# Experts' gates added up by scatters into a zeroed DRAM matrix and multiplied in at the second products, in place of one-hot tables and gate products

## The chip, the cores and the metric

The kernel runs on one core of a Trainium2 chip. The metric is the time of one execution on the device in microseconds (us), the median of several runs. TensorE does the matrix products, VectorE and ACT (ScalarE) the elementwise work, POOL (GpSimd) is almost idle and issues some of the transfers, and SP issues the loads of the weights.

## The reference, cut to what matters

The reference is one transformer block on 256 tokens of width 2048: a gated delta net and a sparse attention side by side, a mixing of the two, and then a layer of 16384 experts (PEER), of which each token uses 16 for each of 8 heads. Only the last part matters here:

```python
qh = (xb @ wq).reshape(TB, PEER_HEADS, PEER_QDIM)
s1 = einsum('thd,hkd->thk', qh[..., :half], keys1)     # 128 scores
s2 = einsum('thd,hkd->thk', qh[..., half:], keys2)     # 128 scores
v1, i1 = top_k(s1, 16); v2, i2 = top_k(s2, 16)
cand = v1[..., :, None] + v2[..., None, :]             # 16 x 16
sc, pos = top_k(cand, 16)
eidx = i1 * 128 + i2, taken at pos                     # which of 16384 experts
gw = softmax(sc)                                       # the gates
act = gelu(einsum('td,thkd->thk', xb, u[eidx]))
out = einsum('thk,thkd->td', gw * act, v[eidx])
```

The kernel gathers no experts. It computes the first product of every token with all 16384 experts, the gelu of each, multiplies by a matrix of gates G (zero for an expert that a token doesn't use, the sum of the gates where two heads choose the same one), and multiplies the result with all of `v`.

## The kernel before

An expert has the number 128 i + j. The first products run in 128 groups j: a group is the 128 experts i on the partitions and 256 tokens in the columns, and its sum over 2048 is 48 matmuls (`stat256`; each weight is split into a high and a low part in a format of TensorE, three products for each of 16 slices). The gelu of group j goes to `at_j(j)`, a piece of 128 x 256 of the big tile `A` (two tiles, groups 0 to 79 and 80 to 127). The second products read `A` as weights (`w_split` cuts each group into `wh` and `wl`) and stream `v`, in two halves of 1024 output columns, 128 groups j in each half, 12 matmuls of 512 columns in a group.

All weights come as 512 KB loads on SP's queue. Each load is cut into two pieces; ACT casts the high part of a piece (`whi`) and VectorE subtracts (`wlo`), up to three pieces ahead of TensorE (class `Stream`). Each engine runs its instructions in the order in which the program writes them. The order around the main loop is made while the program is written out: a class `Background` holds generators (tasks), and `bg.step()`, called after each group of matmuls, lets each task whose time has come write out its next few instructions. The times belong to a simple clock of planned costs (`Times`); a task yields the time at which it wants to go on, a negative value meaning just that time and not at least half a microsecond after its last instruction. At most 8 tasks are active.

Routing is such a task (`route_task`, line 1762): for each head the scores, `top16` on 128 and on 256 values, and after the last head one pass that turns the positions into the numbers i and j of the experts and the scores into gates. Then i, j and gates are transposed (tokens in the columns) with `PE.transpose`, and the gates are split into three bf16 parts.

`gate_task` (line 1854) makes the matrix of gates on TensorE, four tokens at a time. VectorE builds for each token two tables of 128 x 128 bf16: `oi`, which has a one where the choice (on the partitions) has the number i, and `ow`, the same for j, times the three parts of the gate. Three matmuls for each token sum `oi` against `ow` into 128 x 128 gates in PSUM. `put` multiplies them into the groups of `A` that are there already, or stores them in `A` where the group isn't there yet; in that case the gelu goes to a tile `aj`, and VectorE multiplies it in. This runs beside the first products, from the end of routing (about 1340 us) to the end of that stage; `need("gates")` stands behind the loop.

During the second products `g2_task` computes a row of the modulation on VectorE (64 steps of one load and one `SCALAR_TENSOR_TENSOR` of 512 columns), and then loads it, `x1` and the last norm's weights on POOL's queue.

All instructions that go through the timing wrapper carry its line, 289, in the profile; they are told apart by the names of their tiles.

Of the kernel before, what the change touches and what calls it, by code (L numbers as in the profile page):

```python
# [18 lines left out]
T = 256  # L19
# [48 lines left out]
def _const_array():  # L68
    t = np.arange(128)
    ch = t // 64  # L70
    same = ch[:, None] == ch[None, :]
    parts = []

    def add(name, a):
        a = np.asarray(a, np.float32).reshape(128, -1)
        _CONSTS[name] = (sum(p.shape[1] for p in parts), a.shape[1])
        parts.append(a)

    add("ident", np.eye(128))
    add("iota", np.repeat(t[None, :], 128, 0))  # L80
    add("sel", t % 32 == 0)
    add("one", np.ones(128))
    add("ones", np.ones((128, 128)))
    add("tri", same & (t[:, None] <= t[None, :]))
    add("same", same)
    add("ind0", np.repeat((t < 64)[:, None], 128, 1))
    add("ind1", np.repeat((t >= 64)[:, None], 128, 1))

    i, j = t[:, None] % 64, np.arange(64)[None, :]
    add("identc", i == j)  # L90

    add("inclTd", (ch[:, None, None] == np.arange(2)[None, :, None]) & (i[:, :, None] <= j[:, None, :]))
    for l in range(6):
        b = 1 << l
        add(f"lev{l}", (i // (2 * b) == j // (2 * b)) & (i // b % 2 == 1) & (j // b % 2 == 0))
    add("causal", np.where(t[None, :] <= t[:, None], 0.0, NEG))
    n = np.arange(16)
    for tb in range(2):
        add(f"cmpm{tb}", np.where(16 * n[None, :] + 31 <= (t + 128 * tb)[:, None], 0.0, NEG))
    add("cmpv", np.stack([t >= 31, t + 128 >= 31], 1))  # L100
    add("selc", t[:, None] % 32 == np.arange(32)[None, :])
    half = 16
    inv = (np.float32(500000.0) ** (-np.arange(half, dtype=np.float32) / np.float32(half))).astype(np.float32)
    add("inv", np.repeat(inv[None, :], 128, 0))
    return np.concatenate(parts, 1)
# [74 lines left out]
NPAIR = 3  # L180
WO = [(512 * j, 512) for j in range(4)]
# [224 lines left out]
def _build(nc, tc, A, out, stacks, dump, at, stop_at):  # L406
# [33 lines left out]
    bg = Background(times, 8, lambda: "first" in done and next(ada_gen, None), lambda: PACE2 if "o7" in done else PACE)  # L440
# [108 lines left out]
    crowd = dram.tile([1, D], F32, name="crowd")  # L549

# [701 lines left out]
    bg.add(pre_task())  # L1252
    def kc_task():
        yield from kv_rot(c0, 64, kcT[:, 0], 1)
        done.add("kc")
# [455 lines left out]
    sp = pool(st_A, "sp", side=RIGHT)  # L1711
    st_e = stack()
# [23 lines left out]
    eqs = [qs_[:, 1024 * i:1024 * i + 1024] for i in range(2)]  # L1736
# [9 lines left out]
    gate = tmp(256)  # L1746
    eidx = tmp(512).rearrange("p (w b n) -> p w b n", w=2, b=2)

    ij = [ep.tile([128, T], BF, name=f"ij{n}") for n in range(2)]
    gs = [ep.tile([128, T], BF, name=f"gs{n}") for n in range(3)]  # L1750
    iota4 = ep.tile([128, 128, 4], BF, name="iota4")
    V.tensor_copy(iota4, C("iota")[:, :, None].to_broadcast([128, 128, 4]))
# [9 lines left out]
    def route_task():  # L1762
# [24 lines left out]
        V.tensor_copy(iif, ii)  # L1787
        V.tensor_scalar(au, posu, 4, None, op0=OP.logical_shift_right)
        V.tensor_copy(af[:, 0], au)
        V.tensor_scalar(au, posu, 15, None, op0=OP.bitwise_and)  # L1790
        V.tensor_copy(af[:, 1], au)
        yield bg.now() + RPACE
        for tb in range(2):
            for w in range(2):
                for h0 in (0, 4):
                    hs_ = slice(h0, h0 + 4)
                    eq = eqs[w].rearrange("p (h s k) -> p h s k", h=4, s=16)
                    V.tensor_tensor(eq, af[:, w, tb, hs_, :, None].to_broadcast([128, 4, 16, 16]),
                                    C("iota")[:, None, None, 0:16].to_broadcast([128, 4, 16, 16]), OP.is_equal)
                    yield bg.now() + RPACE  # L1800
                    V.tensor_tensor(eq, eq, iif[:, tb, w, hs_, None, :].to_broadcast([128, 4, 16, 16]), OP.mult)
                    yield bg.now() + RPACE
                    V.tensor_reduce(eidx[:, w, tb, :].rearrange("p (h s) -> p h s", h=8)[:, hs_], eq, axis=AX.X,
                                    op=OP.add)
                    yield bg.now() + RPACE
        for tb in range(2):
            V.tensor_tensor(gw[:, tb], scv[:, tb], scv[:, tb, :, 0:1].to_broadcast([128, 8, 16]), OP.subtract)
        yield bg.now() + RPACE
        act(gw, gw, AF.Exp)
        yield bg.now() + RPACE  # L1810
        sm = vv[:, 0, 0, :, 0:2].rearrange("p h b -> p b h")
        V.tensor_reduce(sm, gw, axis=AX.X, op=OP.add)
        V.reciprocal(sm, sm)
        V.tensor_tensor(gw, gw, sm[:, :, :, None].to_broadcast([128, 2, 8, 16]), OP.mult)
        yield bg.now() + RPACE
        for dst, src in zip((*ij, gate), (eidx[:, 0], eidx[:, 1], gw.rearrange("p b h s -> p b (h s)"))):
            S.copy(dst, transpose_to(ps(), src, 2).rearrange("p b t -> p (b t)"))
            yield bg.now() + RPACE
        for n in range(3):
            V.tensor_copy(gs[n], gate)  # L1820
            if n < 2:
                V.tensor_tensor(gate, gate, gs[n], OP.subtract)
        done.add("gate")
# [26 lines left out]


    j_there, t_there = 0, 0

    def gate_task():
        nonlocal t_there
        nt = 4
        yield from wait_for("gate")
        ones, sums = {}, {}
        start, steps = bg.now(), 0
        pace = ((128 - j_there) * 5.15 - GEND) / (4 * T / nt)  # L1860

        def pause():
            nonlocal steps
            steps += 1
            return start + steps * pace

        def make(t0):
            oi = ep.tile([128, 128, nt], BF, name="oi", bufs=2)
            ow = ep.tile([128, 3, 128, nt], BF, name="ow", bufs=2)
            over = lambda a: a[:, None, t0:t0 + nt].to_broadcast([128, 128, nt])  # L1870
            V.tensor_tensor(ow[:, 2], iota4, over(ij[1]), OP.is_equal)
            V.tensor_tensor(oi, iota4, over(ij[0]), OP.is_equal)
            yield -pause()
            for n in range(3):
                V.tensor_tensor(ow[:, n], ow[:, 2], over(gs[n]), OP.mult)
            ones[t0] = oi, ow

        def products(t0):
            oi, ow = ones.pop(t0)
            p = ps()  # L1880
            for t in range(nt):
                for n in range(3):
                    PE.matmul(p[:, 128 * t:128 * t + 128], oi[:, :, t], ow[:, n, :, t], start=n == 0, stop=n == 2)
            sums[t0] = p

        def put(t0):
            nonlocal t_there
            pv = sums.pop(t0).rearrange("p (t j) -> p j t", t=nt)
            for q, (a, b) in enumerate(((0, JA), (JA, 128))):
                m = min(max(j_there, a), b)  # L1890
                x = act_by[q][:, :, t0:t0 + nt]
                if m > a:
                    V.tensor_tensor(x[:, :m - a], x[:, :m - a], pv[:, a:m], OP.mult)
                if m < b:
                    S.copy(x[:, m - a:], pv[:, m:b])
            t_there = t0 + nt

        yield from make(0)
        yield pause()
        for t0 in range(0, T, nt):  # L1900
            if t0 + nt < T:
                yield from make(t0 + nt)
                yield -pause()
            if t0:
                put(t0 - nt)
            yield pause()
            products(t0)
            yield pause()
        put(T - nt)
        done.add("gates")  # L1910

    bg.add(gate_task())
    for j in range(128):
        if j == JA:
            need("gate")
        p = ps()
        for i in range(4):
            h, l = stream.get()
            stat256(p[:, :T], h, l, 4 * i, 4)
        a = at_j(j)  # L1920
        n = t_there
        if n:
            t = ep.tile([128, T], F32, name="aj", bufs=2)
            act(t[:, :n], p[:, :n], AF.Gelu_apprx_tanh)
            V.tensor_tensor(a[:, :n], a[:, :n], t[:, :n], OP.mult)
        if n < T:
            act(a[:, n:], p[:, n:T], AF.Gelu_apprx_tanh)
        j_there = j + 1
    need("gates")
# [5 lines left out]
    vp_ = lambda: hp.tile([128, 1024], F32, name="ht")  # L1935
    ssf = sp.tile([128, 2, 4], F32, name="ssf")
# [10 lines left out]
    def g2_task():  # L1947
# [5 lines left out]
        for m, v in enumerate(ada_late((G2,), lambda q: crow[q // 2][:, q % 2 * 512:q % 2 * 512 + 512],  # L1953
                                       small[:, 0:64].rearrange("p (n q) -> p n q", q=4), small[0:16, 128:256],
                                       lambda m: room[:, m % 2 * 512:m % 2 * 512 + 512])):
            yield max(start + G2PACE * m, v or 0.0)
# [7 lines left out]
    bg.add(g2_task())  # L1964

# [59 lines left out]
    V.memset(ssf, 0.0)  # L2025
    ws = [w_split(j) for j in range(AHEAD)]
    for half in range(2):
        accs = [[ps() for c in range(2)] for tb in range(2)]
        for j in range(126 if half else 128):
            w = ws.pop(0)  # L2030
            if j + AHEAD < 128 or half == 0:
                ws.append(w_split((j + AHEAD) % 128))
            for n in range(2):
# [42 lines left out]
```

## Time and profile before

| | |
|---|---|
| median of 3 runs | 2703.28 us (2698.82 to 2706.44) |
| profiled execution | 2697.54 us, its span 2695.8 us |
| busy, share of the span | TensorE 98%, VectorE 73%, ACT 52%, POOL 1% |
| granted clock of TensorE | 0.995 of full speed |
| moved by DMA | 571.15 MB, 212 GB/s over the span |

The profile is that of one execution. A busy TensorE is counted from a matmul's start to its modelled end, so overlapping matmuls count once. "Idle before" is the time that an engine stood still ahead of an instruction, with what ended it. The time of a transfer is that from its issue to its landing.

### The profile page before, as it was taken

What the parts mean: (1) busy time and instruction counts of PE and PEld (TensorE: products, weight loads), DVE (VectorE), ACT (ScalarE), POOL (GpSimd) and SP (SyncE); (2) the same over time, 40 slices, a digit from 0 to 9 for tenths busy, and PEclk for the clock granted to TensorE, in tenths of its full rate; (3) what the DMA queues carried; (4) which work ended last, traced back from release to release, by engine and by line L of the source; (5) the groups of instructions that cost most, each with busy time, mean ns of one, the idle gap of its engine ahead of it and who ended that gap; (6) DMA issues with size and microseconds to landing.
All of it is one profiled execution on the core that took longest, in us unless ns stands there. A gap on an engine that the chain in (4) does not pass through costs nothing.

```text
span 2695.8 us, 46915 instructions
## 1 busy us (share of the span) xinstructions
PE 2648.1 (98%) x17004; PEld 2278.1 (85%) x17004; DVE 1958.4 (73%) x4378; ACT 1393.3 (52%) x2983; POOL 36.6 (1%) x83
## 2 busy tenths in 40 slices
PE   8999999999999999999999999999999999999998
PEld 5777777777877778999999999999988888788886
DVE  6667877767777777999866666677577777766666
ACT  4446756565555445454544444444455555555555
POOL 0001000000000000000000000000000000000000
PEclk9999999999999999999999999999999999999999
DMA  9886756666676885555544444444577777765554
GB/s 348 310 313 229 243 174 199 197 225 229 226 241 234 291 311 200 177 173 187 185 160 152 155 157 157 153 157 155 179 256 235 235 234 235 251 193 189 188 188 157
DMA packets 176921, 571.15 MB, mean 212 GB/s; under 512 B 20048, under 2 KB 20384, under 8 KB 176176
## 3 DMA queue, kind: packets, MB, share of 16 engines
q1 hardware_dynamic: 168336, 538.21, 60.5%
q0 software_dynamic: 6624, 23.65, 2.5%
q10 hardware_dynamic: 1728, 6.29, 0.6%
q8 instruction: 133, 2.18, 0.3%
q14 instruction: 100, 0.82, 0.1%
HBM read 554.94 MB, written 13.13 MB: 211 GB/s over the span
## 4 chain that ended last, share of the span: by engine, by line
PE 91%; DVE 4%; ACT 2%; DMA 2%; issue 1%; ACTq 0%; DVEq 0%; POOLq 0%
PE ps L289 91%; DVE wlo L289 1%; DMA adas<-ada_t 1%; ACT whi L289 1%; DVE adas L289 0%; DMA raw<-w_in 0%; DVE cv L289 0%; ACT L289 0%; DVE ht L289 0%; DMA ccom<-consts 0%; DVE x L289 0%; ACT gsq L289 0%; DVE big L289 0%; ACT mix L289 0%; ACT o L289 0%
## 5 line engine op out<-in xcount | busy, mean ns | idle before, releaser
L289 DVE TENSOR_TENSOR wlo<-raw,whi 128x512 fp32r<-128x512 f32 (+2 forms) x1632 | 1098.2, 685 | 509.6 <-ACT whi L289 476.9
L289 ACT CAST whi<-raw 128x512 fp32r<-128x512 f32 (+2 forms) x1632 | 994.4, 618 | 772.7 <-PE ps L289 600.6
L289 PE MATMUL ps<-ht,whi 128*128 128x256 f32 x4608 | 828.8, 282 | 0.8 <-DVE ht L289 0.8
L289 PEld LDWEIGHTS ps<-ht,whi 128*128 128x128 f32 x4608 | 708.1, 189 | 1.2 <-DVE ht L289 1.0
L289 PE MATMUL ps<-ht,wlo 128*128 128x256 f32 x2304 | 647.2, 281 | 0.0
L289 PE MATMUL ps<-whi,ht 128*128 128x512 f32 (+2 forms) x1536 | 523.0, 403 | 5.0 <-ACT whi L289 3.8
L289 PEld LDWEIGHTS ps<-ht,wlo 128*128 128x128 f32 x2304 | 434.1, 188 | 0.0
L289 PE MATMUL ps<-wlo,wh 128*128 128x512 f32 x1024 | 408.6, 399 | 0.0
L289 PE MATMUL ps<-whi,wh 128*128 128x512 f32 x1024 | 403.7, 394 | 0.8 <-ACT wh L289 0.8
L289 PE MATMUL ps<-whi,wl 128*128 128x512 f32 x1024 | 401.5, 392 | 0.0
L289 PEld LDWEIGHTS ps<-whi,ht 128*128 128x128 f32 x1536 | 289.6, 190 | 87.3 <-issue 10.8
L289 PE MATMUL ps<-wlo,ht 128*128 128x512 f32 (+2 forms) x768 | 300.8, 392 | 3.4 <-DVE wlo L289 3.0
L289 PEld LDWEIGHTS ps<-whi,wh 128*128 128x128 f32 x1024 | 192.2, 188 | 50.8 <-ACT wh L289 1.0
L289 PEld LDWEIGHTS ps<-whi,wl 128*128 128x128 f32 x1024 | 192.2, 188 | 46.3 <-DVE wl L289 0.2
L289 PEld LDWEIGHTS ps<-wlo,wh 128*128 128x128 f32 x1024 | 192.2, 188 | 44.0
L289 PEld LDWEIGHTS ps<-wlo,ht 128*128 128x128 f32 x768 | 146.5, 191 | 32.3 <-DVE wlo L289 8.2
L289 ACT CAST wh<-A 128x256 fp32r<-128x256 f32 x256 | 103.7, 406 | 134.4 <-PE ps L289 134.4
L289 DVE SCALAR_TENSOR_TENSOR adas<-adas,crow 128x512 f32<-128x512 f32 x192 | 131.6, 686 | 43.1 <-DMA adas<-ada_t 42.8
L289 DVE TENSOR_TENSOR wl<-A,wh 128x256 fp32r<-128x256 f32 x256 | 109.0, 427 | 65.7 <-ACT wh L289 65.4
L289 PE MATMUL ps<-ow,oi 128*128 128x128 bf16 x768 | 101.3, 296 | 0.0
L289 ACT COPY A<-ps 128x192 f32<-128x192 f32 (+16 forms) x124 | 34.4, 307 | 114.1 <-DVE A L289 93.3
L289 PEld LDWEIGHTS <-oi 128*128 128x128 bf16 x768 | 81.7, 118 | 3.8
(323 smaller groups left out, 2298.6 us busy)
## 6 DMA issues: line engine op xcount, KB each, us to landing
raw<-u SPq DMA_DIRECT2D x256, 512.0 KB, 3.5
raw<-v SPq DMA_DIRECT2D x256, 512.0 KB, 3.6
raw<-w_in SPq DMA_DIRECT2D x170, 512.0 KB, 4.4
adas<-ada_t SPq DMA_DIRECT2D x192, 256.0 KB, 3.6
raw<-ada_w SPq DMA_DIRECT2D x64, 512.0 KB, 6.5
raw<-wn SPq DMA_DIRECT2D x32, 512.0 KB, 4.9
raw<-wo SPq DMA_DIRECT2D x32, 512.0 KB, 4.9
raw<-wq SPq DMA_DIRECT2D x32, 512.0 KB, 3.5
```

The source lines that it names most:

```text
L289: r = f(*args, **kw)
```

## The change

A DRAM matrix `gated[tb]` of 128 i x 128 j x 128 tokens takes the place of the tables, one for each block of 128 tokens. A new background task, `zero_task`, fills both with zeros from a zeroed tile, in 64 writes of 256 KB on ACT's queue, 5 us of the planner's clock apart. Nine tasks may be active.

Routing now finishes two heads at a time (`settle`, `NSET = 2`): numbers, gates, and for each choice its place (i x 128 + j) x 128 + token. Then `indirect_dma_start` on POOL's queue adds one gate for each of the 128 tokens of a block to its place, 32 choices x 2 blocks after each two heads, 256 in all. The transposes, the three bf16 parts, `gate_task` and its tables are gone, and each gelu goes straight to `A`.

Ahead of the second products `gates_load` starts to load the gates of two groups j at a time on POOL's queue (two loads of 128 KB, three tiles in turn). In their first half `gate_mult` multiplies them into two groups of `A` on VectorE, one to two groups ahead of `w_split`, and issues the load for six groups on. `g2_task` yields a fixed next time, at least 2 us later, instead of one behind its last instruction.

```diff
+ZPACE = 5.0
+NGT = 3
+NSET = 2
-    bg = Background(times, 8, lambda: "first" in done and next(ada_gen, None), lambda: PACE2 if "o7" in done else PACE)
+    bg = Background(times, 9, lambda: "first" in done and next(ada_gen, None), lambda: PACE2 if "o7" in done else PACE)
+    gated = [dram.tile([128, 128, 128], F32, name=f"gated{tb}") for tb in range(2)]
+    def zero_task():
+        zero = per.tile([128, 512], F32, name="zero")
+        V.memset(zero, 0.0)
+        for js in range(0, 128, 4):
+            for g in gated:
+                S.dma_start(g[:, js:js + 4].rearrange("i j t -> i (j t)"), zero)
+                yield bg.now() + ZPACE
     bg.add(pre_task())
+    bg.add(zero_task())
...
+    def gates_load(j):
+        g = sp.tile([128, 2, 2, 128], F32, name="gates2", bufs=NGT)
+        for tb in range(2):
+            G.dma_start(g[:, tb], gated[tb][:, j:j + 2])
+        gates_of.append(g)
...
+            if h % NSET == NSET - 1:
+                yield from settle(slice(h - NSET + 1, h + 1))
+                done.add(f"settled{h}")
+        done.add("gate")
+    def settle(hs_):
...
+        for tb in range(2):
+            for w in range(2):
+                eq = eqs[w].rearrange("p (h s k) -> p h s k", h=NSET, s=16)
+                V.tensor_tensor(eq, af[:, w, tb, hs_, :, None].to_broadcast([128, NSET, 16, 16]),
+                                C("iota")[:, None, None, 0:16].to_broadcast([128, NSET, 16, 16]), OP.is_equal)
+                V.tensor_tensor(eq, eq, iif[:, tb, w, hs_, None, :].to_broadcast([128, NSET, 16, 16]), OP.mult)
+                V.tensor_reduce(eidx[:, w, tb, :].rearrange("p (h s) -> p h s", h=8)[:, hs_], eq, axis=AX.X,
+                                op=OP.add)
+                yield bg.now() + RPACE
...
+        i, j = eidx[:, 0, :, ns], eidx[:, 1, :, ns]
+        V.scalar_tensor_tensor(i, i, 128.0, j, op0=OP.mult, op1=OP.add)
+        V.tensor_scalar(i, i, 128.0, C("tcol"), op0=OP.mult, op1=OP.add)
+        V.tensor_copy(place[:, :, ns], i)
         yield bg.now() + RPACE
-        for dst, src in zip((*ij, gate), (eidx[:, 0], eidx[:, 1], gw.rearrange("p b h s -> p b (h s)"))):
-            S.copy(dst, transpose_to(ps(), src, 2).rearrange("p b t -> p (b t)"))
-            yield bg.now() + RPACE
...
+        for n in range(ns.start, ns.stop):
+            for tb in range(2):
+                nc.gpsimd.indirect_dma_start(
+                    gated[tb].rearrange("i j (t o) -> (i j t) o", o=1),
+                    bass.IndirectOffsetOnAxis(ap=place[:, tb, n:n + 1], axis=0),
+                    gate[:, tb, n:n + 1], None, compute_op=OP.add)
...
-    def gate_task():
...
-    bg.add(gate_task())
     for j in range(128):
...
-        a = at_j(j)
-        n = t_there
-        if n:
-            t = ep.tile([128, T], F32, name="aj", bufs=2)
-            act(t[:, :n], p[:, :n], AF.Gelu_apprx_tanh)
-            V.tensor_tensor(a[:, :n], a[:, :n], t[:, :n], OP.mult)
-        if n < T:
-            act(a[:, n:], p[:, n:T], AF.Gelu_apprx_tanh)
-        j_there = j + 1
-    need("gates")
+        act(at_j(j), p[:, :T], AF.Gelu_apprx_tanh)
     st_e.close()
...
+    for j in range(0, 2 * NGT, 2):
+        gates_load(j)
...
-            yield max(start + G2PACE * m, v or 0.0)
+            yield -max(start + G2PACE * m, bg.now() + 2.0, v or 0.0)
...
+    def gate_mult(j):
+        a = act_by[j >= JA][:, j - JA * (j >= JA):j - JA * (j >= JA) + 2, :].rearrange("p j (b t) -> p b j t", b=2)
+        V.tensor_tensor(a, a, gates_of[j // 2], OP.mult)
+        if j + 2 * NGT < 128:
+            gates_load(j + 2 * NGT)
...
+    gate_mult(0)
+    gate_mult(2)
     ws = [w_split(j) for j in range(AHEAD)]
     for half in range(2):
...
             if j + AHEAD < 128 or half == 0:
                 ws.append(w_split((j + AHEAD) % 128))
+            if half == 0 and j % 2 and j + 3 < 128:
+                gate_mult(j + 3)
```

## Rows read from the trace of the kernel before

**Rows 1.** The page: busy times by engine, and the chain of waits.

```profile
PE 2648.1 (98%) x17004; PEld 2278.1 (85%) x17004; DVE 1958.4 (73%) x4378; ACT 1393.3 (52%) x2983; POOL 36.6 (1%) x83
...
PE 91%; DVE 4%; ACT 2%; DMA 2%; issue 1%; ACTq 0%; DVEq 0%; POOLq 0%
```

**Rows 2.** Stretches: length, busy us and starts by engine, clock, DMA share, GB/s.

```profile
50.00:100.00 50.00, 49.84 (x325) 35.55 (x325) 33.53 (x64) 19.42 (x36) 0.00 (x0) 1.00 0.93 357
205.00:570.00 365.00, 352.17 (x2661) 275.23 (x2661) 279.09 (x791) 228.32 (x548) 10.03 (x30) 0.98 0.64 208
1150.00:1250.00 100.00, 100.00 (x849) 100.00 (x849) 92.65 (x302) 49.94 (x92) 0.00 (x0) 1.00 0.56 177
1250.00:1340.00 90.00, 90.00 (x763) 90.00 (x763) 74.09 (x109) 47.31 (x86) 0.00 (x0) 1.00 0.59 188
1340.00:1440.00 100.00, 100.00 (x847) 99.33 (x847) 65.72 (x146) 45.00 (x107) 0.00 (x0) 1.00 0.49 158
1967.00:2324.00 357.00, 356.94 (x1530) 287.04 (x1531) 269.25 (x511) 198.34 (x385) 0.00 (x0) 1.00 0.73 240
```

**Rows 3.** Groups by form: count, busy us, mean ns, idle time before.

```profile
L289 DVE TENSOR_TENSOR wlo<-raw,whi 128x512 fp32r<-128x512 f32 x1600 | 1083.9, 689 | 502.4 <-ACT whi L289 470.0 <-PE ps L289 0.3
...
L289 PE MATMUL ps<-ow,oi 128*128 128x128 bf16 x768 | 101.3, 296 | 0.0
...
L289 DVE TENSOR_TENSOR ow<-ow,gs 128x512 bf16<-128x512 bf16 x192 | 75.4, 421 | 2.2
...
L289 DVE TENSOR_TENSOR oi<-iota,ij 128x512 bf16<-128x512 bf16 x64 | 26.8, 419 | 0.0
```

**Rows 4.** Timeline of TensorE: start, duration in us, instruction.

```profile
1894.79 1.58 PE L289 MATMUL ps<-ow,oi 128*128 128x128 bf16 x12
1896.12 0.48 PE L289 MATMUL ps<-ht,whi 128*128 128x256 f32 x2
```

**Rows 5.** Tile A: ns min/median/max, first and last start in us.

```profile
L289 ACT CAST wh<-A x256: 388/406/407, 1966.6 to 2677.0; 128x256 fp32r<-128x256 f32 x128
...
L289 DVE MAX8 A<-A x96: 284/295/429, 1082.7 to 1252.2; 128x8 f32<-128x128 f32 x64, 128x8 f32<-128x256 f32 x32
...
L289 DVE TENSOR_TENSOR A<-A,ccom x8: 1217/1219/1223, 1257.6 to 1316.1; 128x1024 f32<-128x1024 f32 x8
...
L289 PE MATMUL ps<-ccom,A x6: 270/272/273, 1331.5 to 1337.0; 128*128 128x128 f32 x6
```

**Rows 6.** Timeline of POOL, as rows 4, with the idle time before.

```profile
205.71 0.50 POOL L289 DMA_DIRECT2D crowd<-crow  x1
...
1962.22 1.06 POOL L289 DMA_DIRECT2D ht<-crowd  x2 [890.47 <-PE ps L289]
```

**Rows 7.** Tile mixd, as rows 5: writes on ACT's queue.

```profile
L289 ACTq DMA_DIRECT2D mixd<-mix x12: 326/326/347, 476.9 to 846.0; - x12
```

**Rows 8.** DMA issues: count, KB each, median us from issue to landing.

```profile
x1d<-x POOLq DMA_DIRECT2D x8, 256.0 KB, 3.7
ht<-x1d POOLq DMA_DIRECT2D x4, 512.0 KB, 10.3
...
cw<-cw POOLq DMA_DIRECT2D x1, 256.0 KB, 5.8
...
modr<-adarow POOLq DMA_DIRECT2D x1, 8.0 KB, 3.8
modr<-ht POOLq DMA_DIRECT2D x1, 8.0 KB, 1.6
```

**Rows 9.** Tile ht in the second products, as rows 5.

```profile
L289 DVE SCALAR_TENSOR_TENSOR ht<-ht x64: 684/684/686, 1977.2 to 2325.7; 128x512 f32<-128x512 f32 x64
```

**Rows 10.** What TensorE waited for: us in total, times, longest.

```profile
PE ps L289 <- ACT wh L289: 0.8, 1, 0.8
```

**Rows 11.** Timeline of VectorE beside POOL's issues, as rows 4.

```profile
1961.58 0.69 DVE L289 TENSOR_TENSOR wlo<-raw,whi 128x512 fp32r<-128x512 f32 x1
1962.61 0.69 DVE L289 TENSOR_TENSOR wlo<-raw,whi 128x512 fp32r<-128x512 f32 x1 [0.34 <-ACT whi L289]
```

More of the change, by code (lines that the diff above doesn't have):

```diff
@@ L82, in _const_array @@
     add("one", np.ones(128))
+    add("tcol", t)
     add("ones", np.ones((128, 128)))
@@ L1711, in _build @@
     sp = pool(st_A, "sp", side=RIGHT)
+    gates_of = []
+    def gates_load(j):
[3 more added lines that the diff above has]
+        gates_of.append(g)
     st_e = stack()
@@ L1735, in _build @@
     qhs = [qs_[:, 256 * i:256 * i + 256] for i in range(16)]
-    eqs = [qs_[:, 1024 * i:1024 * i + 1024] for i in range(2)]
+    eqs = [qs_[:, NSET * 256 * i:NSET * 256 * (i + 1)] for i in range(2)]
     work = [[tmp(512) for _ in range(4)]]
@@ L1745, in _build @@
     gw = tmp(256).rearrange("p (b h s) -> p b h s", b=2, h=8)
-    gate = tmp(256)
     eidx = tmp(512).rearrange("p (w b n) -> p w b n", w=2, b=2)
[L1749 to L1752, printed above, removed]
+    place = ep.tile([128, 2, 128], U32, name="place")
+    gate = ep.tile([128, 2, 128], F32, name="gate")
     MIN = -3.0e38
@@ L1786, in route_task @@
                 yield bg.now() + RPACE
[L1787 to L1791, printed above, removed]
+            if h % NSET == NSET - 1:
[3 more added lines that the diff above has]
+    def settle(hs_):
+        V.tensor_copy(iif[:, :, :, hs_], ii[:, :, :, hs_])
+        V.tensor_scalar(au[:, :, hs_], posu[:, :, hs_], 4, None, op0=OP.logical_shift_right)
+        V.tensor_copy(af[:, 0, :, hs_], au[:, :, hs_])
+        V.tensor_scalar(au[:, :, hs_], posu[:, :, hs_], 15, None, op0=OP.bitwise_and)
+        V.tensor_copy(af[:, 1, :, hs_], au[:, :, hs_])
         yield bg.now() + RPACE
@@ L1794, in route_task @@
             for w in range(2):
[L1795 to L1799, printed above, removed]
-                    yield bg.now() + RPACE
[L1801 to L1805, printed above, removed]
+                eq = eqs[w].rearrange("p (h s k) -> p h s k", h=NSET, s=16)
@@ L1806, in route_task @@
         for tb in range(2):
-            V.tensor_tensor(gw[:, tb], scv[:, tb], scv[:, tb, :, 0:1].to_broadcast([128, 8, 16]), OP.subtract)
+            V.tensor_tensor(gw[:, tb, hs_], scv[:, tb, hs_], scv[:, tb, hs_, 0:1].to_broadcast([128, NSET, 16]),
+                            OP.subtract)
         yield bg.now() + RPACE
-        act(gw, gw, AF.Exp)
+        act(gw[:, :, hs_], gw[:, :, hs_], AF.Exp)
         yield bg.now() + RPACE
-        sm = vv[:, 0, 0, :, 0:2].rearrange("p h b -> p b h")
@@ L1812, in route_task @@
-        V.tensor_reduce(sm, gw, axis=AX.X, op=OP.add)
+        ns = slice(16 * hs_.start, 16 * hs_.stop)
+        sm = vv[:, 0, 0, hs_, 0:2].rearrange("p h b -> p b h")
+        V.tensor_reduce(sm, gw[:, :, hs_], axis=AX.X, op=OP.add)
         V.reciprocal(sm, sm)
-        V.tensor_tensor(gw, gw, sm[:, :, :, None].to_broadcast([128, 2, 8, 16]), OP.mult)
-        yield bg.now() + RPACE
-        for dst, src in zip((*ij, gate), (eidx[:, 0], eidx[:, 1], gw.rearrange("p b h s -> p b (h s)"))):
-            S.copy(dst, transpose_to(ps(), src, 2).rearrange("p b t -> p (b t)"))
-            yield bg.now() + RPACE
@@ L1819, in route_task @@
[L1819 to L1823, printed above, removed]
+        V.tensor_tensor(gate[:, :, ns].rearrange("p b (h s) -> p b h s", s=16), gw[:, :, hs_],
+                        sm[:, :, :, None].to_broadcast([128, 2, NSET, 16]), OP.mult)
+        i, j = eidx[:, 0, :, ns], eidx[:, 1, :, ns]
+        V.scalar_tensor_tensor(i, i, 128.0, j, op0=OP.mult, op1=OP.add)
+        V.tensor_scalar(i, i, 128.0, C("tcol"), op0=OP.mult, op1=OP.add)
@@ L1847, in _build @@
             done.add(f"qh{ct // 2}")
-    j_there, t_there = 0, 0
-    def gate_task():
[L1855 to L1910, printed above, removed]
-    bg.add(gate_task())
     for j in range(128):
```

## The prediction

> **What bounds the kernel now.** First the page's busy times and its chain of waits: TensorE is busy 2648.1 of 2695.8 us, and the chain of work that ended last lies on it for 91% [rows 1]. Then the table of stretches, for the two stages that the change touches. While the first products run (the 128 groups j of `stat256`, about 1145 to 1966 us), TensorE has no idle time and starts 849 matmuls per 100 us before the gates' products begin, 847 once they are mixed in; VectorE is busy 92.7% in one of these stretches and TensorE loses nothing by it. In the second products, the half that will carry the new multiplications (1967 to 2324 us) has TensorE busy 356.9 of 357 us, VectorE 269.3, ACT 198.3, DMA 0.73 [rows 2]. So a matmul taken out of the first stage is worth its slot, and work taken off VectorE or ACT there is worth nothing; work added to VectorE in the second stage costs nothing as long as the cover holds.
>
> **What goes.** The gates' products are 768 matmuls of 128x128 bf16 [rows 3]. Their slot is read from the stretches: 847 starts in 100 us without idle time give 0.118 us for each matmul, of either kind [rows 2], so 768 x 0.118 = 90.7 us. One group of 12 began at 1894.79 us and the matmul behind it at 1896.12, 0.111 us each [rows 4], which would give 85; the group's busy column says 101.3 [rows 3], but there modelled ends lie over the next matmul. I take 90.7, with 85 and 101 as ends. The six transposes of gates and indices [rows 5] go too, 6 x 0.118 = 0.7 us. On VectorE the tables and gate products (x192, x64 for `oi` and as many for `ow`, at 0.42 us: 134 us) [rows 3] and the multiplications from PSUM go; by the above that is worth 0.
>
> **What is added, in the order in which it runs.**
>
> Zeroing: 64 writes of 256 KB, issued on ACT's queue, one per 5 us of the planner's clock, from where the setup loads on POOL's queue stand now (205.7 us) [rows 6]. A write issued there takes ACT 0.326 us [rows 7], so 64 x 0.326 = 20.9 us of ACT, in a stretch (205 to 570 us) where ACT is busy 228 and TensorE 352 of 365 us, DMA 0.64 [rows 2]. Ends: 0, if ACT's free 137 us take them, and 21, if each one delays TensorE's chain. ACT is mostly free, so nearer to 0: I take +3. The ninth place among the background tasks shifts the order of work in this stage, to either side; I allow 5 us for it.
>
> Routing: `settle` runs four times instead of once. It is the same comparison, product and sum over 16 candidates, 48 operations of 512 elements instead of 24 of 1024 (1.22 us each) [rows 5]. The nearest row for the half width is 0.689 us [rows 3], so 33 us instead of 29, and there are some 40 small ones, taken at no more than the 0.28 us of the shortest MAX8 [rows 5]: about +10 us of VectorE over 250. Three of 512 elements are now issued back to back (2.1 us); a `top16` already is five operations of up to 0.43 us [rows 5]. Cost on TensorE between 0 and 8 us; +1.
>
> Scatters: 256 on POOL's queue, 128 elements of 4 bytes each. POOL had been idle for 890 us at 1962.22 [rows 6], so nothing is queued behind them but the gates' loads. A scatter that adds into a matrix must find the sums of the one before, so I expect each to wait until the last one on its own matrix has landed; two matrices alternate, which makes 128 steps of one landing time each. Nothing in this trace is a scatter. Nearest rows: POOL's two small writes to DRAM land after 1.6 and 3.8 us, its 256 KB writes after 3.7; the far end is 10.3 us for 512 KB reads [rows 8]. I take 3.7, as two of the three rows of writes have about that. Start: first and last MAX8 are at 1082.7 and 1252.2 us [rows 5], so a head takes 21.3 us, the second head ends at 1125 and its settle some 20 us later: 1145. Then 1145 + 128 x 3.7 = 1619 us. The second products begin at 1966.6 now (first cast to `wh`) [rows 5], then at 1966.6 - 91.4 = 1875; less 5.8 us for a load of gates (256 KB on POOL's queue) [rows 8] the sums are due at 1869. Cover: 250 us. It is gone at (1869 - 1145) / 128 = 5.7 us per step.
>
> The Trainium skill, DMA: Bandwidth & Descriptors, section "Anatomy of one DMA — SWDGE (gpsimd) path", puts the fixed part of such a DMA at about 2.0 us; by that (an estimate) the chain takes 256 us, and the sum stays as it is. Rows 8 are mostly higher, and I go by them.
>
> Gates' loads: 128 of 128 KB on POOL's queue, 0.53 us of POOL each (1.06 for two) [rows 6], two for every 5.6 us of the first half. Three buffers give some 16 us of lead against 5.8 to 10.3 us to land [rows 8]. DMA goes from 0.73 by 16.8 MB in 357 us (47 on 240 GB/s) to about 0.87, where 0.93 with 357 GB/s left TensorE at 49.84 of 50 us [rows 2]. Taken as 0.
>
> Multiplications: 64 on VectorE, 128x512 f32, 0.689 us each as the split has it [rows 3]: 44 us, so 269 + 44 = 313 of 357, 88%. The G2 task may now run faster than its 5.5 us per step (64 steps from 1977.2 to 2325.7) [rows 9]; at 4.75 us VectorE stands at about 90% for 305 us. The cover is the stretch with 92.7% and a full TensorE [rows 2]. Ends: 0 and 44; I take +1. At the stage's start the first multiplications can run before the last gelu ends, so the 0.8 us that TensorE waits there for `wh` [rows 10] stays.
>
> **Sum.** -90.7 - 0.7 + 3 + 1 + 1 = -86.4 us. The profiled execution took 2697.5 us (span 2695.8), so 2611. The median of the three runs is 2703.3, 5.7 us above it, and I carry that over: 2617 us. What a measurement of this kernel can tell from no change is about 0.3%, 8 us. With the ends of the slot (85 to 101), of the zeroing (0 to 21) and the planner's 5 us, the forecast's own range is 2602 to 2635.
>
> **Rivals.**
>
> (a) The chain of scatters sets the start of the second products. One mechanism, on POOL's queue: while sums are missing the loads of gates wait, VectorE waits for the first load, and TensorE for VectorE. It decides from 5.7 us per step; with a step of P the whole takes 2617 + 128 (P - 5.7). At 6.4 us the gain is gone. At 7 us: 2783; if both matrices make one chain of 256 at 3.7 us (7.4 per step): 2835. For it: no scatter is in this trace, 10.3 us exists as a landing time [rows 8], and 128 separate elements may land later than one block. Against: all the rows of writes are under 4 us. Chance 0.12 that no gain is left (0.10 beyond 0.3%), 0.04 for a delay that leaves some.
>
> (b) VectorE's cover breaks where it is thinnest, in the routing. From 1145 to 1340 us some 53 steps, 106 scatters, run beside a VectorE with about 23 us free (7.4 per 100 us, later 15.9 of 90) [rows 2]. If each scatter kept VectorE out for as long as POOL takes for a plain issue (0.53 us), that is 56 us, and with the 10 us of settle 43 more than there is: 2660 us. A sign against: at 1962.22 POOL issued two loads in 1.06 us, and the split that VectorE began at 1962.61 took 0.69 us, as the one before it did [rows 6, 11]. But these loads read no indices. Chance 0.11.
>
> The Trainium skill, SBUF — State Buffer, section "Who interferes with whom", has this as a rule: a VectorE instruction with two SBUF inputs and a GpSimd instruction that reads SBUF shut each other out for the whole instruction. The split has two such inputs. Rows 11 agree only in so far as a plain issue doesn't shut it out; no run here shows an issue that reads indices.
>
> (c) The zeroing lies on the path whole: 18 us over the forecast, 2635. For it: TensorE already has 13 us idle in 205 to 570 us, so chains over other engines do reach it there [rows 2]. Against: ACT is 63% busy there. Chance 0.06.
>
> (d) The multiplications in the second products lie on the path whole, by late loads or a full VectorE: 43 over the forecast, 2660. Against: the cover worked out above. Chance 0.05.
>
> That leaves 0.62 for the forecast. Faster by over 0.3% are the forecast, (b), (c), (d) and the part of (a) that leaves a gain: 0.88. The rest of (a) gives 0.10 for slower and 0.02 between. The range for 8 in 10, 2600 to 2662, takes in (b) to (d) and leaves most of (a) out.
>
> **What would show it.** The first products end near 1875 us with the same 849 matmuls per 100 us, and no matmul of `oi` and `ow` is left. POOL shows 256 scatters, the last one well before that end (near 1619 us by my step); if they lie further apart than 5.7 us per pair, and the first multiplication waits for a load, (a) is right. Splits longer than 0.69 us beside scatters, and TensorE under 849 per 100 us up to 1340 us, would be (b); the stage before 570 us longer by more than 5 us, (c); TensorE idle in the first half of the second products, (d). I am wrong above all if a scatter's landing time is far from that of a plain write.

## The result, and the profile after

The changed kernel takes 2619.03 us (median of 4 runs, 2615.24 to 2621.55) against 2702.89 us for the kernel before in the same rounds (2698.82 to 2706.44): a ratio of 0.9689, 95% interval 0.9670 to 0.9708. Forecast were 2617 us and a range of 2600 to 2662. The profiled execution after took 2620.39 us (span 2618.6).

The page after, its busy times and the chain of waits, which answer to [rows 1]:

```profile
span 2618.6 us, 45489 instructions
PE 2561.6 (98%) x16230; PEld 2191.3 (84%) x16230; DVE 1833.5 (70%) x3998; ACT 1383.1 (53%) x2810; POOL 525.2 (20%) x467
PE 86%; DVE 7%; ACT 3%; DMA 3%; issue 2%; ACTq 0%; DVEq 0%; SPq 0%; POOLq 0%
```

TensorE lost 774 matmuls, 768 + 6, and 86.5 us of busy time, and it bounds the kernel as before. POOL went from 36.6 to 525.2 us. The chain has 5 points less of TensorE and 3 more of VectorE, so some new waits reach the end.

Stretches of the kernel after, columns as in [rows 2] (length, busy us and starts of TensorE, its weight loads, VectorE, ACT and POOL, clock, DMA share, GB/s): the zeroing, the routing with scatters, the first products with scatters, and the first half of the second products.

```profile
205.00:570.00 365.00, 350.85 (x2646) 272.89 (x2645) 275.89 (x783) 226.27 (x543) 10.02 (x30) 0.98 0.74 242
1150.00:1250.00 100.00, 99.85 (x843) 99.48 (x843) 86.18 (x250) 53.82 (x95) 61.56 (x38) 1.00 0.71 178
1370.00:1470.00 100.00, 100.00 (x847) 100.00 (x846) 49.07 (x71) 48.12 (x88) 67.31 (x42) 1.00 0.77 186
1885.00:2243.00 358.00, 352.67 (x1508) 282.70 (x1509) 291.37 (x573) 195.67 (x382) 70.81 (x133) 1.00 0.87 291
```

Beside 38 and 42 scatters per 100 us TensorE is busy 99.85 and 100.00 us, with 843 and 847 starts. The one stretch of the four that is worse than before by more than 2 us is the last: TensorE stands 5.3 of 358 us, where it stood 0.06 of 357 [rows 2]. VectorE is not full there, 291 of 358 us.

The new operations by tile: duration in ns (min/median/max), first and last start.

```profile
L1851 POOL DMA_INDIRECT gated<-gate,place x256: 1541/1543/2073, 1161.2 to 1798.5; - x128
L293 POOL DMA_DIRECT2D gates<-gated x128: 536/537/605, 1801.1 to 2221.2; - x128
...
L293 DVE TENSOR_TENSOR A<-A,gates x64: 679/685/693, 1884.7 to 2236.5; 128x512 f32<-128x512 f32 x64
```

The last scatter starts at 1798.5, not near 1619; the first cast to `wh` is at 1885.4, and the sums were due some 5.8 us before that. From the first scatter to the last a pair takes (1798.5 - 1161.2) / 127.5 = 5.0 us. The timeline of POOL at the start of the chain shows where the pair's time goes (start, duration, instruction, idle time before and what ended it):

```profile
1161.16 1.85 POOL L1851 DMA_INDIRECT gated<-gate,place  x1 [80.52 <-DVE place L293]
1163.31 1.56 POOL L1851 DMA_INDIRECT gated<-gate,place  x1 [0.30 <-issue]
1166.28 1.55 POOL L1851 DMA_INDIRECT gated<-gate,place  x1 [1.41 <-DMA gated<-gate,place]
```

The second scatter goes out at once, on the other matrix; the third waits for the first to have landed. Issuing one takes POOL 1.54 us or more, three times a plain load (0.537 us).

By stage, from the first matmul of one to the first of the next in both traces:

| stage | before, us | after, us | difference | forecast |
|---|---|---|---|---|
| start to the first scores of the routing | 1079.03 | 1087.93 | +8.9 | +3 |
| to the first second product | 888.03 | 797.96 | -90.07 | -90.7 - 0.7 + 1 = -90.4 |
| to the end | 728.7 | 732.7 | +4.0 | +1 |
| sum | 2695.8 | 2618.6 | -77.2 | -86.4 |

The medians differ by 83.9 us. With -90.07 and +4.0 that leaves +2.2 for the first stage; the rest of its +8.9 is the two profiled executions (the one before lay 5.3 us under its median, the one after 1.4 above). In the traces of all runs here the first stage took 1079.0 to 1085.4 us in the kernel before and its variants, and 1079.5 to 1087.9 in the kernel after and its own, so two traces alone say little on it.

### The profile page after: what moved, and what is told of

It is laid out like the page before. It is cut to its first block, busy times and chain, and to the rows that moved or that the text cites. A ratio compares the mean times of both kernels' runs of the same rounds, so it can differ in the third digit from the quotient of the medians.

```text
span 2618.6 us, 45489 instructions
## 1 busy us (share of the span) xinstructions
PE 2561.6 (98%) x16230; PEld 2191.3 (84%) x16230; DVE 1833.5 (70%) x3998; ACT 1383.1 (53%) x2810; POOL 525.2 (20%) x467
## 4 chain that ended last, share of the span: by engine, by line
PE 86%; DVE 7%; ACT 3%; DMA 3%; issue 2%; ACTq 0%; DVEq 0%; SPq 0%; POOLq 0%
PE ps L293 86%; DVE wlo L293 2%; DMA adas<-ada_t 2%; ACT whi L293 1%; DVE adas L293 1%; DVE A L293 1%; ACT L293 0%; DMA ht<-ada_t 0%; DVE cv L293 0%; DMA raw<-w_in 0%; ACT o L293 0%; DVE ht L293 0%; ACT gsq L293 0%; DMA ccom<-consts 0%; DVE x L293 0%
## 5 line engine op out<-in xcount | busy, mean ns | idle before, releaser
L293 PE MATMUL ps<-ht,whi 128*128 128x256 f32 x4608 | 820.1, 281 | 0.8 <-DVE ht L293 0.8
L1851 POOL DMA_INDIRECT gated<-gate,place x256 | 420.3, 1642 | 299.1 <-DMA gated<-gate,place 183.0
L293 DVE SCALAR_TENSOR_TENSOR adas<-adas,crow 128x512 f32<-128x512 f32 x192 | 131.5, 685 | 36.6 <-DMA adas<-ada_t 36.1
L293 POOL DMA_DIRECT2D gates<-gated x128 | 68.4, 539 | 343.4 <-DVE A L293 331.7
L293 ACT ACTIVATE A<-ps 128x256 f32<-128x256 f32 x128 | 49.3, 385 | 112.3 <-PE ps L293 112.0
```

Source lines behind the costliest of these rows:

```text
L293: r = f(*args, **kw)
L1851: nc.gpsimd.indirect_dma_start(gated[tb].rearrange("i j (t o) -> (i j t) o", o=1), bass.IndirectOffsetOnAxis(ap=place[:, tb, n:n + 1], axi ...
```

## The experiments

The leading theory after this result: the gain is the TensorE slots alone, scatters and zeroing are hidden, and the loss in the second products is a wait at their start. Its rivals: the zeroing or the scatters cost something that a larger gain covers; relief of VectorE is part of the gain; the loss at the start is VectorE being full.

**Kernel before with the zeroing alone (e1).**

```diff
+    gated = [dram.tile([128, 128, 128], F32, name=f"gated{tb}") for tb in range(2)]
+    def zero_task(): ...            # as in the change
-    bg = Background(times, 8, ...)
+    bg = Background(times, 9, ...)
+    bg.add(zero_task())
```

> The kernel before with the zeroed DRAM matrix alone: zero_task's 64 writes on ACT's queue, and nine background tasks; nothing reads the matrix. Theory: ACT's issues are mostly hidden, TensorE's first part (up to the routing) gets 3 to 7 us longer, 2703 becomes about 2708. Rival (c): each issue of 0.326 us lies on the path, +21 us, about 2724. Second rival: the 9 us that the changed kernel loses before the routing are the planner's new order or chance and not the writes; then between -5 and +2.

Measured: 2703.67 us against 2702.2, ratio 1.0004 [0.9995, 1.0013], that is +1 us (-1.3 to +3.5). Rival (c), 18 us, falls, and so does the +5 that I still expected here. In this trace the first products and all that follows took 1616.7 us, as before, so the write traffic leaves nothing behind.

**One of three gate products (e2);** the two lower parts of the gates are left out.

```diff
-                for n in range(3):
-                    PE.matmul(..., oi[:, :, t], ow[:, n, :, t], start=n == 0, stop=n == 2)
+                PE.matmul(..., oi[:, :, t], ow[:, 0, :, t], start=True, stop=True)
```

> The kernel before with one of the three gate products for each token (256 matmuls for 768; the two lower parts of the gates are left out), VectorE's tables and products unchanged. Theory: a matmul here costs a slot of 0.118 us whatever its columns, 512 x 0.118 = -60 us, 2643. Rival: it costs by its columns (128 for 256), half of that, -30 us, 2673. Second rival: the busy column is right (101.3 us for 768), -67.5 us, 2635.

Measured: 2639.08 us, 0.9774 [0.9759, 0.9789], 61 to 63 us less. From its first score to its first second product it took 827.43 us, 60.60 less than before: 512 matmuls at 0.118 us are 60.4. So the slot read from starts per 100 us is the price, not the group's busy column (0.132 us each, 67.5), and not half a slot for half the columns (30).

**Tables built once (e3).** VectorE is spared the tables and gate products of all tokens but the first eight, so the gates of the others are left out; TensorE's matmuls stay.

```diff
+            if t0 >= 2 * nt:
+                yield -pause()
+                ones[t0] = kept[t0 % (2 * nt)]
+                return
...
-            ones[t0] = oi, ow
+            ones[t0] = kept[t0] = oi, ow
```

> The kernel before with VectorE's tables built for the first 8 tokens only and used again for all others (the gates of the others are left out); all 768 matmuls stay. VectorE loses 62 x 5 = 310 operations of 0.42 us, 130 us, in a stage where TensorE has no idle time. Theory: worth nothing, 2703 within 3 us. Rival: the gain of the change came in part from the relief of VectorE; then several us faster, up to 2690 or less.

Measured: 2700.36 us, 0.9999 [0.9990, 1.0008], and 888.03 us for the first products, the same to 0.01 us. Some 310 VectorE operations less are worth nothing there.

**One DRAM matrix for both token blocks (e4),** so that all 256 scatters make one chain.

```diff
-    gated = [dram.tile([128, 128, 128], F32, name=f"gated{tb}") for tb in range(2)]
+    both = dram.tile([2, 128, 128, 128], F32, name="gated")
+    gated = [both[tb] for tb in range(2)]
...
+        V.tensor_scalar(i[:, 1], i[:, 1], 128.0 ** 3, None, op0=OP.add)
...
-                    gated[tb].rearrange("i j (t o) -> (i j t) o", o=1),
+                    both.rearrange("b i j (t o) -> (b i j t) o", o=1),
```

> The changed kernel with both blocks in one DRAM matrix, so that each of the 256 scatters adds into the matrix of the one before. Theory of rival (a): a scatter waits until the one before on its matrix has landed. Landing takes 4.3 us (median in the trace of the changed kernel), with some 0.4 us to start again 4.7 us per scatter: 256 x 4.7 = 1203 us from 1161, so the second products start near 2370 instead of 1885 and the whole takes about 3100 us. Rival: POOL's own 1.64 us per scatter sets the step and the two matrices don't matter; then 2619, no change.

Measured: 2988.07 us, 1.1066 [1.1049, 1.1084], 369 us above the changed kernel; some 3100 us were expected, with 4.7 us per scatter where 4.26 came out. What engines waited for in it (us in total, times, longest):

```profile
POOL gated L1853 <- DMA gated<-gate,place: 666.5, 254, 5.4
...
PE ps L293 <- ACT wh L293: 369.8, 1, 369.8
```

TensorE stands once, for 369.8 us, on the first cast of the second products, and behind it are the loads of gates and POOL's queue. That is rival (a), made on purpose. Its formula, 2617 + 128 (P - 5.7), with P twice the mean step read from this trace, (2245.2 - 1159.9) / 255 = 4.26 us, gives 2977 against the 2988 measured. Two stretches of this kernel, columns as above, one while first products run and one while TensorE stands:

```profile
1570.00:1670.00 100.00, 100.00 (x848) 100.00 (x847) 49.10 (x71) 48.33 (x88) 33.89 (x20) 1.00 0.68 185
2100.00:2200.00 100.00, 0.00 (x0) 0.00 (x0) 0.00 (x0) 0.00 (x0) 46.71 (x31) 0.50 0.13 0
```

20 scatters in 100 us beside 185 GB/s of other traffic, 31 without: a step of 5.0 us against 3.2. A scatter lands after 5.1 us on the median in the first stretch and after 3.0 in the second, and its issue takes POOL 1.77 and 1.54 us on the mean. The weights stream only in the first, but VectorE and ACT work only there too; that the streaming alone makes the difference is not shown.

**No scatters (e11);** the gates stay zero and everything else stays.

```diff
-        for n in range(ns.start, ns.stop):
-            for tb in range(2):
-                nc.gpsimd.indirect_dma_start(gated[tb]..., compute_op=OP.add)
```

> The changed kernel without the 256 scatters (the gates stay zero; all else runs). Theory: they are hidden but for the 1 us per 100 us that TensorE starts fewer matmuls beside the routing, 2616 to 2618. Rival (b): an issue of 1.5 to 2 us that reads indices keeps VectorE out; then tens of us faster, 2580 or less.

Measured: 2617.47 us (2616.92 to 2618.71), 0.9683 [0.9668, 0.9699], against 2619.03 and 2618.29 for the kernel with them; 797.17 us for the first products against 797.96. By the medians the 256 scatters cost 0.8 to 1.6 us, by the stage 0.8; the interval reaches some 4 us to either side. Rival (b), 43 us, falls.

**The changed kernel again (e5), the zeroing in 16 larger writes (e7), G2's first step later (e6), and both (e8).** The wait at the start of the second products stands in the waits of the kernel after, TensorE's and VectorE's:

```profile
PE ps L293 <- DVE wlo L293: 4.4, 3, 2.9
...
DVE ht L293 <- DMA ht<-ada_t: 8.5, 4, 5.5
```

`ht<-ada_t` is the weight of a G2 step. The step's VectorE instruction is placed before its load has landed, and the splits `wlo` that TensorE needs stand behind it in order. (The expectation of e6 put the wait down to the row of the condition on POOL's queue; the profile names `ada_t`, and e10 below tells the two apart.) The timeline of VectorE shows the longest of these waits:

```profile
1890.17 0.69 DVE L293 TENSOR_TENSOR wlo<-raw,whi 128x512 fp32r<-128x512 f32 x1
...
1896.38 0.69 DVE L293 SCALAR_TENSOR_TENSOR ht<-ht 128x512 f32<-128x512 f32 x1 [5.53 <-DMA ht<-ada_t]
```

and TensorE's shows what it does with it:

```profile
1894.42 0.40 PE L293 MATMUL ps<-whi,wh 128*128 128x512 f32 x1
1897.74 0.50 PE L293 MATMUL ps<-wlo,wh 128*128 128x512 f32 x1 [2.92 <-DVE wlo L293]
```

Theory: the planner places G2's first steps too close behind the issue of their loads; 10 us of its clock later, the wait is gone.

```diff
-        start = bg.now()
+        start = bg.now() + 10.0
```

For the zeroing, fewer and larger writes:

```diff
-        for js in range(0, 128, 4):
+        for js in range(0, 128, 16):
...
-                yield bg.now() + ZPACE
+                yield bg.now() + 4 * ZPACE
```

> The changed kernel once more, as the base for the three kernels beside it: 2619 us.

> The changed kernel with G2's first VectorE step 10 us of the planner's clock later. In its trace VectorE stands 5.5 us at the start of the second products, in front of G2's first step, and TensorE then stands 2.9 us: the row of the condition is loaded on POOL's queue, and that load now stands behind four loads of gates that wait for the first multiplications. Theory: those 4 to 5 us come back, 2614 to 2615. Rival: they belong to VectorE being too full (81% in this half); then no change, 2619.

> The changed kernel with the zeroing in 16 writes of 1 MB (the zeroed tile repeated by the access pattern), 20 us of the planner's clock apart: the same bytes, a quarter of ACT's issues. Theory: what zeroing costs is ACT's issue time on the path, so 2 to 5 us come back, 2614 to 2617. Rival: it costs by its bytes in the DMA queues; no change, 2619.

> The changed kernel with both edits, the later G2 step and the zeroing in 16 writes. Theory: the two add up, -6 to -10 us, 2609 to 2613. Rival: neither matters, 2619.

Measured: again 2618.29 us (2612.37 to 2620.17), 0.9689 [0.9676, 0.9702]; G2 later 2610.74 (2609.79 to 2612.63), 0.9663 [0.9649, 0.9676]; 16 writes 2616.41 (2611.7 to 2619.18), 0.9681 [0.9668, 0.9695]; both 2611.30, 0.9663 [0.9649, 0.9676]. The delay of G2 is worth 7.5 us by the medians, more than the 4 to 5 expected. All ten runs of the two kernels with the later G2 lie at 2609.8 to 2612.6 us, the nine of the kernel as made at 2612.4 to 2621.6. In the trace its second products take 728.3 us against 732.7 after, and of the waits of TensorE from 1870 to 2240 us only one is left:

```profile
PE ps L293 <- ACT wh L293: 1.0, 1, 1.0
```

so 4.4 us of the 7.5 are seen in that stage; the other 3 lie within what whole executions differ by. The 16 writes bring 2 us, less than can be told apart, and nothing beside the later G2. The later G2, alone or with the 16 writes, is the fastest of the versions run: 8 us under the change as made, and 91 under the kernel before.

**The old form of the wait in G2 (e9), and G2's loads issued ahead of the first multiplications (e10).** Theory A: steps are placed before their loads can land, and it is the changed yield that does it. Theory B: POOL's queue is at fault, where loads of gates stand ahead of G2's own `crowd` loads.

```diff
-            yield -max(start + G2PACE * m, bg.now() + 2.0, v or 0.0)
+            yield max(start + G2PACE * m, v or 0.0)
```

```diff
+    bg.step()
     gate_mult(0)
```

> The changed kernel with g2_task's old yield (a step is written out behind the planned end of the last one, and the first behind the planned landing of its loads). Both theories are on why the later G2 step gave 7 us. Theory A: the new yield puts G2's first steps on VectorE before their loads are there; with the old one they stand 10 us behind the stage's start and the time is that of the later step, 2611. Theory B: the order on POOL's queue makes the row's load late, the yield doesn't matter; 2618.

> The changed kernel with g2_task's first part (its loads on POOL's and SP's queues) written ahead of the first multiplications, so that the row's load stands before the loads of gates that wait for VectorE; G2's first VectorE step then also stands some 2 us earlier. Theory A (the steps are put before their loads can be there): no gain, 2618 or more. Theory B (POOL's order): 2611 to 2614.

Measured, e10: 2618.79 us, 0.9689 [0.9676, 0.9703]. G2's `crowd` load goes out 5.0 us before the stage instead of 1.9 after its start, and VectorE waits all the same. The first load of `ada_t` goes out 8.9 us before the step that needs it can start (8.3 in the kernel after). VectorE's waits in this stage, and TensorE's:

```profile
PE ps L293 <- DVE wlo L293: 3.4, 2, 2.3
...
DVE ht L293 <- DMA ht<-ada_t: 5.3, 1, 5.3
```

B falls: the load that is late is the weight `ada_t` on SP's queue, not one of POOL's. e9: 2620.15 us, 0.9691 [0.9677, 0.9704], where I expected 2611. Half of theory A holds: with the old form VectorE has no such wait at the start. But G2 now ends too late. TensorE's timeline at the end of the first half:

```profile
2241.80 0.40 PE L293 MATMUL ps<-whi,wl 128*128 128x512 f32 x1
2247.26 0.38 PE L293 MATMUL ps<-ccom,mcol 128*16 128x128 f32 x1 [5.07 <-DVE mcol L293]
2247.30 0.77 PE L293 MATMUL ps<-whi,wh 128*128 128x512 f32 x1
2247.87 0.63 PE L293 MATMUL ps<-wlo,wh 128*128 128x512 f32 x1
```

The last of the 64 steps starts at 2246.0, and the matmul that sums G2 (`ccom,mcol`), placed by order ahead of the second half, holds TensorE for 5.07 us. The kernel before had 1.11 us at this place (2325.78 to 2326.89). The pace is not slower than there, (2246.0 - 1903.6) / 63 = 5.4 us per step against 5.5, but the first step stands 20.7 us behind the stage's start where it stood 10.1, and the last two steps wait 1.4 and 1.2 us for their loads. So in this kernel the old form places the first step too late for its pace; the new one starts early and takes 4.4 us per step, and what it lacked was a late enough start. e6 starts 10 planner's us later and ends at 2194.4 us, 46 us ahead of the half's end.

## Why the prediction was right, step by step

**The slot.** -90.7 and -0.7 against -90.07 for the stage, with settle and scatters in it. e2 decided between the three prices (0.111, 0.118 and 0.132 us per matmul) for the middle one. Where TensorE is without idle time here, starts per 100 us are the price of a matmul; busy columns count modelled ends that overlap.

**VectorE's relief at 0.** Confirmed by e3: there VectorE is busy 1855.2 us instead of 1958.4, and 103 us less bought nothing.

**The zeroing at +3.** About +1 by e1; inside its bounds of 0 to 21. The DMA share rose from 0.64 to 0.74 in 205 to 570 us, and TensorE's idle time there from 12.8 to 14.2 us.

**Routing and settle at +1, no lock with scatters.** Held. In e11 the stage is 888.03 - 797.17 = 90.9 us shorter than in the kernel before; against the 91.4 of the slots that leaves 0.5 us for the routing, and 0.8 for the scatters. VectorE's split `wlo` took 688 ns on the mean of 396 in the kernel before between 1161 and 1800 us, and 690 of 447 in the kernel after, beside all scatters. The Trainium skill, SBUF — State Buffer, section "Who interferes with whom", has a VectorE instruction with two SBUF inputs and a GpSimd instruction that reads SBUF shut each other out. These issues do read indices, and the trace shows no such thing at the size of a split: 2 ns on the mean. On POOL's side an issue took 1.64 us on the mean in the kernel after, and 1.54 in e4 while VectorE stood; the loads and the other engines stood then too, so the cause of that tenth stays open.

**The scatters' step at 3.7 us per pair.** The term that was mis-sized: 5.0 us after, and (1837.3 - 1157.1) / 127.5 = 5.3 in e6. The first one started at 1161, not 1145 (9 of these 16 us are the longer first stage of this trace). Where I had put a cover of 250 us there were (1885.9 - 5.8) - (1798.5 + 4.3) = 77, and in e6, worked out likewise from 1881.5 and 1837.3, 34; the point from which it decides, 5.7, is close. The order of the argument held (hidden, and from 5.7 us on 128 us for each us more, which e4 bears out), the distance did not, and that a step a third longer than mine still stayed hidden is in part luck. Two things were wrong. POOL's own time for an issue was left out; the page after has it:

```profile
L1851 POOL DMA_INDIRECT gated<-gate,place x256 | 420.3, 1642 | 299.1 <-DMA gated<-gate,place 183.0
```

Of the 639 us from the first scatter to the end of the last, POOL issues for 420 and waits for landings for 183. Two issues of 1.54 us, each with 0.30 us behind it, make 3.7 us per pair before any wait (that this equals the forecast is chance), so by this estimate the chain would not have ended before 1161 + 128 x 3.7 = 1635 us however fast a scatter lands. And I had taken the landing time of plain writes without asking what runs beside them: a scatter lands after 4.3 us on the median in the kernel after, and in e4 after 5.1 beside the first products and 3.0 with nothing beside it. Issues on POOL's queue after: count, KB each where the trace has it, median us to landing.

```profile
gates<-gated POOLq DMA_DIRECT2D x128, 128.0 KB, 4.7
...
gated<-gate,place POOLq DMA_INDIRECT x256, 4.3
```

The Trainium skill, DMA: Bandwidth & Descriptors, section "Anatomy of one DMA — SWDGE (gpsimd) path", with its 2.0 us of fixed time, would by an estimate (1161 + 128 x 2.0) have put the chain's end near 1417 us. The shortest median landing that a run here showed, 3.0 us, is above that time.

**The gates' loads at 0.** Held: VectorE waited 0.8 us for them in all of the first half, and the DMA share came out at 0.87, as worked out.

**Multiplications at +1, "the G2 task may now run faster".** The stage lost 4.0 us. The cover was there: the 64 multiplications took 43.8 us, but VectorE's busy time rose from 269 to 291 us only, mostly since rows that follow one another at once overlap by 0.08 us and count once. The loss came from the part named in half a sentence: the steps of G2 were reordered, and of a step that moves I did not follow the load to its landing. e6 takes the loss away with the multiplications in place, so it is not theirs, and rival (d) falls with its 43 us.

**The sum and the chances.** By the medians the three stages came out 0.8 us under, 0.3 over and 3.0 over their terms. The forecast's own range, 2602 to 2635, is narrower than the ends that it names added up, some 2599 to 2646. Rivals (b), (c) and (d) are refuted, and (a) is right as a mechanism, with a chain that ends some 180 us later than I put it. 0.12 for no gain by (a) was not too much for a cover that turned out this thin.

## What to carry to other kernels

Price a removed matmul by starts per time in a stretch without idle time. For a chain of DMAs that wait for each other, price what one takes of the issuing engine as well as its landing beside the work of the stage where it will run, and compare the whole chain with its due time, since beyond it every step counts in full. After an edit that changes when background steps are placed, look at both ends of their stage: too early, and an in-order engine waits for a load with critical work behind it; too late, and the sum at the end holds TensorE.

## What the hardware showed unexpectedly

A wait of TensorE can cost more than its length. In the second run of the changed kernel the wait at the start came out as follows on TensorE's timeline, and the stretch from 1888.8 to 1891 us shows the granted clock (0.50, ahead of the DMA share and GB/s):

```profile
1885.42 0.40 PE L293 MATMUL ps<-whi,wh 128*128 128x512 f32 x1
1888.32 0.73 PE L293 MATMUL ps<-wlo,wh 128*128 128x512 f32 x1 [2.50 <-DVE wlo L293]
1888.85 0.63 PE L293 MATMUL ps<-whi,wl 128*128 128x512 f32 x1
1889.27 0.63 PE L293 MATMUL ps<-whi,wh 128*128 128x512 f32 x1
```

```profile
1888.80:1891.00 2.20, 2.20 (x7) 1.66 (x6) 2.20 (x6) 0.21 (x1) 0.00 (x0) 0.50 1.03 412
```

Until 1891.8 us matmuls start 0.43 us apart instead of 0.233, at a granted clock of 0.50, the lower of its two levels (1.2 of 2.4 GHz). Eight of them at 0.19 us more add some 1.6 us to the 2.5 waited. The same follows the wait of 5.07 us in e9 above (starts at 2247.30, then 2247.87 and every 0.43 us until 2252.14), about 2 us more. In the kernel after, the longest wait of 2.92 us was not followed by it: starts come 0.23 us apart from 1898.08 on, and the clock reads 1.00. Of the five traces with this wait at the start of the second products four show the lower clock behind it (waits of 2.1, 2.3, 2.5 and 3.3 us in e7, e10, e5 and e11), and only the kernel after does not, so the length of the wait alone does not decide; what does stayed open.
